# Third attention layer: queries and keys in two rounded parts, scores as three rounded products

## The chip, the cores and the metric

The kernel runs on one core of a Trainium2 chip. The metric is the time of one execution on the device in microseconds (us). The engines are TensorE (PE, with its weight loads as PEld), VectorE (DVE), ScalarE (ACT), GpSimd (POOL) and SyncE (SP), which issues most DMAs. Each engine works through its own queue in order.

## What is computed

The reference is two blocks one after the other on a sequence of 512 tokens with 1024 features. The first merges a state-space branch, a gated recurrence and an attention over a memory; the second is a chain of four layers, of which the third is a latent attention (`mla_branch`), the one that is changed. Cut to what matters:

```python
def mla_branch(h, w_in, q_norm, kv_norm, w_uq, w_ukv, w_out):      # 16 heads
    c_q, c_kv, k_rope, z = split(h @ w_in, [768, 1024, 1056])
    q  = (rmsnorm(c_q, q_norm) @ w_uq)      # per head 64 plain + 32 rope columns
    kv = (rmsnorm(c_kv, kv_norm) @ w_ukv)   # per head 64 key + 64 value columns
    q = concat(q[..., :64], rope(q[..., 64:]))
    k = concat(kv[..., :64], rope(k_rope) for every head)          # 96 wide
    o = causal_attention(q, k, kv[..., 64:], scale=96 ** -0.5)
    return (o * silu(z)) @ w_out
```

The scores are causal: query block n (128 queries) sees (n + 1) * 128 keys, so a head has four score tiles of 128 x 128, 128 x 256, 128 x 384 and 128 x 512.

## The kernel before, in words

The whole program is one Python trace; a scheduler puts each engine's instructions into an order by their place in the program and by what is ready. Large products are made with rounded operands: a value is copied by ACT into a rounded type (`fp32r`, the high part) and DVE subtracts that from the value to get the low part; the product is then high x high + high x low + low x high. For weights this is `wsplit` (L311 to L323): `wfetch` (L302) loads 128 x 1024 into one of three staging buffers `wf`, ACT casts into `wh` (L317), DVE subtracts into `wl` (L318). There are seven pairs `wh`/`wl`, taken in turn through the counter `nw`, so a cast waits until PE has finished with the weights of seven loads before. For activations it is `split` (L467; without a scale the copy is L471 and the subtraction L472). All matmuls that are not transposes go through the helper `mm` (L272), so their line is L277 (L275 when an order is asked for). Plain two-tensor operations of this layer go through the helper `tt`, so their line is L1803.

PSUM has four banks `g` (products and scores, handed out in turn by `gb`) and four banks `t` (transposes, probabilities times values). The working memory has 36 slots of 128 x 512 fp32 (`st`, `Slots`), handed out first in, first out, and eight rounded tiles `rt`.

The third attention layer is `mla` (L1801). Its part in front makes the latents, the rotated shared key `kr`, and two sets of key tiles `kt[s][e]` (s: even or odd head pair, e: head of the pair) in `st` slots: POOL clears 32 unused rows, ACT copies the rope rows (L1855 to L1858). Then 8 head pairs c follow. `up(c)` makes the pair's keys (`w_uk`, ACT copies at L1883 and L1884 empty the bank), for every even c a rope tile of two pairs (`w_uq[8 + t]`; two products with the rope tables and a shuffle on DVE, L1892), and the queries (`w_uq[c]`, ACT copies at L1901, and DVE adds the two rope halves into the query tile). `scores(c)` makes per head four fp32 matmuls query x key into the `g` banks, DVE adds the causal mask and takes the maximum (L1936), ACT takes the exponential (L1940), DVE normalises (L1943). One head's four scores are eight fp32 records. `core(c)` transposes the probabilities of pair c (L1959, copied at L1961), makes the scores of pair c + 1 in between, and multiplies with the values. `weave` mixes `core(c)` with fillers: the gate product of the pair (`gate`, 24 matmuls of 512 columns, L1236 and L1237 empty its bank), `up(c + 2)`, and once the second half of the values. After pair 7 the output projection `layer_out("w_co")` takes eight weight loads.

## Time and profile before

| | |
|---|---|
| median of 3 runs | 1915.02 us (1912.07 to 1915.43) |
| profiled execution, its own time | 1914.73 us |
| its span, first to last instruction | 1913.0 us |
| PE busy | 1863.3 us (97%) |
| PE weight loads busy | 1515.8 us (79%) |
| DVE busy | 1299.9 us (68%) |
| ACT busy | 893.1 us (47%) |
| POOL busy | 60.4 us (3%) |
| mean granted TensorE clock | 0.996 of full speed |

Busy time of an engine is the time covered by its instructions. Matmuls are pipelined: a record's end is modelled and reaches over the start of the next one, so the spacing of starts says what PE is held for, and the length of one record says more than that. An fp32 matmul leaves two records, a rounded one leaves one. A timeline row merges several records of one kind: its length goes from the start of the first to the end of the last, and the shape is that of the first. "Idle before" is the time in which an engine did nothing in front of an instruction, and the arrow names what ended it.

### The profile page before, as it was taken

How to read it: one execution, taken by the hardware profiler on the slowest of the kernel's cores; microseconds unless marked ns; L12 is line 12 of the kernel's file. 1: busy time of each engine (PE TensorE's matmuls, PEld its weight loads, DVE VectorE, ACT ScalarE, POOL GpSimd, SP SyncE). 2: the span in 40 equal slices, each digit the busy share in tenths (PEclk: the TensorE clock that was granted, in tenths of full speed). 3: DMA queues.
4: the chain of work that ended last, by engine and by line, in shares of the span. 5: the costliest groups of instructions: out<-in, count | busy, mean ns of one | idle time of the engine just before them, and what ended most of it. 6: DMA issues, size and time to landing. Idle time of an engine off the chain costs nothing. (4 is left out here: it accounts for less than half of the span.)

```text
span 1913.0 us, 26324 instructions
## 1 busy us (share of the span) xinstructions
PE 1863.3 (97%) x9843; PEld 1515.8 (79%) x9843; DVE 1299.9 (68%) x2579; ACT 893.1 (47%) x1666; POOL 60.4 (3%) x93
## 2 busy tenths in 40 slices
PE   8999999999999999999999999999999999999998
PEld 7778787888888788778778888888887677788887
DVE  7776777757467797765655965787664776758553
ACT  5554545454376644432334454465544555534231
POOL 0010001100000000000001010000000000000000
PEclk9999999999999999999999999999999999999999
DMA  5343324323332436533469554232323122333421
GB/s 184 106 136 97 120 96 121 116 68 118 88 102 82 129 124 204 188 103 119 159 233 309 152 191 130 66 120 77 102 100 100 53 64 67 99 121 110 133 77 44
DMA packets 99202, 229.91 MB, mean 120 GB/s; under 512 B 18081, under 2 KB 38977, under 8 KB 99074
## 3 DMA queue, kind: packets, MB, share of 16 engines
q1 hardware_dynamic: 86192, 216.85, 35.5%
q0 software_dynamic: 2544, 6.00, 1.1%
q10 hardware_dynamic: 10338, 5.38, 1.0%
q8 instruction: 77, 1.26, 0.3%
q14 instruction: 51, 0.42, 0.1%
HBM read 200.28 MB, written 26.35 MB: 118 GB/s over the span
## 5 line engine op out<-in xcount | busy, mean ns | idle before, releaser
L277 PE MATMUL g<-rt,wh 128*128 128x512 f32 (+1 forms) x3664 | 1097.4, 382 | 7.0 <-ACT rt L471 4.2
L277 PEld LDWEIGHTS g<-rt,wh 128*128 128x128 f32 x3664 | 669.0, 189 | 141.0 <-ACT st L1940 5.3
L277 PE MATMUL g<-rt,wl 128*128 128x512 f32 (+1 forms) x1816 | 682.0, 380 | 0.0
L317 ACT CAST wh<-wf 128x1024 fp32r<-128x1024 f32 (+2 forms) x300 | 301.0, 1011 | 469.0 <-PE g L277 337.9
L318 DVE TENSOR_TENSOR wl<-wf,wh 128x1024 fp32r<-128x1024 f32 (+2 forms) x300 | 349.8, 1173 | 241.9 <-ACT wh L317 228.1
L277 PEld LDWEIGHTS g<-rt,wl 128*128 128x128 f32 x1816 | 343.2, 189 | 63.2 <-issue 2.2
L277 PE MATMUL g<-wh,rt 128*128 128x512 f32 x992 | 310.2, 393 | 0.9 <-DVE rt L475 0.7
L277 PEld LDWEIGHTS g<-wh,rt 128*128 128x128 f32 x992 | 185.8, 189 | 40.5 <-DVE rt L475 1.0
L277 PE MATMUL g<-wl,rt 128*128 128x512 f32 x496 | 193.4, 390 | 0.0
L277 PEld LDWEIGHTS g<-wl,rt 128*128 128x128 f32 x496 | 93.1, 188 | 19.5 <-issue 0.3
L277 PE MATMUL t<-st 128*64 128x64 f32 (+8 forms) x746 | 76.8, 274 | 8.0 <-DVE st L720 3.8
L665 DVE SCALAR_TENSOR_TENSOR st<-g,pc,st 128x511 f32<-128x511 f32 (+2 forms) x108 | 80.0, 745 | 5.6 <-ACT st L662 5.0
L1260 DVE TENSOR_TENSOR st<-st 128x512 f32<-128x512 f32 (+4 forms) x180 | 76.5, 468 | 6.7 <-PE t L1415 5.5
L275 PE MATMUL t<-st 128*64 128x128 f32 (+4 forms) x788 | 72.9, 299 | 4.9 <-ACT st L708 4.9
L275 PEld LDWEIGHTS t<-st 128*64 128x64 f32 (+1 forms) x788 | 55.0, 145 | 20.0 <-issue 10.5
L277 PEld LDWEIGHTS t<-st 128*64 128x64 f32 (+3 forms) x746 | 44.3, 142 | 32.0 <-issue 18.0
L1196 DVE TENSOR_TENSOR st<-g,st 128x512 f32<-128x512 f32 x32 | 22.0, 689 | 60.1 <-ACT st L1195 59.9
L277 PE MATMUL g<-st 128*128 128x256 f32 (+2 forms) x192 | 56.5, 426 | 5.5 <-DVE st L1237 2.4
L744 ACT ACTIVATE st<-st 128x128 f32<-128x128 f32 x128 | 41.8, 394 | 37.2 <-POOL st L740 37.2
L474 ACT ACTIVATE rt<-st 128x512 fp32r<-128x512 f32 x52 | 35.5, 712 | 49.9 <-DVE st L1621 16.3
L720 DVE TENSOR_TENSOR st<-st,t 128x512 f32<-128x512 f32 x68 | 45.2, 681 | 17.0 <-issue 5.8
L1195 ACT ACTIVATE st<-g 128x512 f32<-128x512 f32 x32 | 19.1, 596 | 76.3 <-PE g L277 76.3
(301 smaller groups left out, 1836.7 us busy)
## 6 DMA issues: line engine op xcount, KB each, us to landing
wf<-in_w_xbc SPq DMA_DIRECT2D x24, 512.0 KB
wf<-in_w_gt SPq DMA_DIRECT2D x24, 512.0 KB
wf<-in_w_z SPq DMA_DIRECT2D x16, 512.0 KB
st<-acsD SPq DMA_DIRECT2D x32, 256.0 KB
wf<-in_w_bs SPq DMA_DIRECT2D x16, 512.0 KB
wf<-in_w_lx SPq DMA_DIRECT2D x12, 512.0 KB
wf<-in_w_lg SPq DMA_DIRECT2D x12, 512.0 KB
wf<-in_w_bl SPq DMA_DIRECT2D x16, 384.0 KB
```

Of the source, the lines that this page charges most:

```text
L275: r = self.nc.tensor.matmul(out=out, lhsT=lhsT, rhs=rhs, start=start, stop=stop)
L277: r = self.nc.tensor.matmul(out=out, lhsT=lhsT, rhs=rhs, start=start, stop=stop)
L317: a = nc.scalar.copy(wh, wf)
L318: b = nc.vector.tensor_tensor(out=wl, in0=wf, in1=wh.bitcast(F32), op=ALU.subtract)
L474: nc.scalar.activation(hi, src, AF.Copy if isinstance(scale, float) else AF.Identity, scale=scale)
L665: nc.vector.scalar_tensor_tensor(out=out[:, d:], in0=ps[:, :512 - d], scalar=pcs(f"{n}w{j}", t), in1=out[:, d:], op0=ALU.mult, op1=ALU.add)
L720: tt = lambda o, a, b, op: nc.vector.tensor_tensor(out=o, in0=a, in1=b, op=op)
L744: nc.scalar.activation(m[:, j * P:(j + 1) * P], m[:, j * P:(j + 1) * P], AF.Exp, bias=self.nacs[:, c, h:h + 1])
L1195: nc.scalar.activation(y[:, c], ps, AF.Square, scale=1.0 / 32, accum_out=ss[:, i, n:n + 1])
L1196: nc.vector.tensor_tensor(out=y[:, c], in0=ps, in1=pg[n], op=ALU.mult)
L1260: tt = lambda o, a, b, op: V.tensor_tensor(out=o, in0=a, in1=b, op=op)
```

## The change

The keys and queries of the third attention layer are no longer fp32 tiles in `st` slots. Each is kept as a high and a low rounded part. The place for them is taken from the ring of weight buffers: the counter `nw` becomes a list `W` of pairs, four pairs are taken off its front when the key tiles are made and put back after the last pair of heads, and the other three pairs serve the weight loads in between. Pair s of the lent ones holds the two heads' keys of set s (high part in `wh`, low part in `wl`, 512 columns for each head), pairs 2 and 3 the queries, which so also have two sets in place of slots taken as needed. All copies into them become `split` (a copy on ACT and a subtraction on DVE); the rope halves are added once for two pairs, in place, and then split into each query tile. Each score becomes three rounded matmuls into one bank: high x high, query high x key low, query low x key high.

```diff
--- before.py
+++ after.py
@@ -219,7 +219,8 @@
         self.wf = [p.tile([P, 1024], F32, name=f"wf{j}") for j in range(self.NWF)]
         self.wh = [p.tile([P, 1024], F32R, name=f"wh{j}") for j in range(self.NWS)]
         self.wl = [p.tile([P, 1024], F32R, name=f"wl{j}") for j in range(self.NWS)]
-        self.nw = self.nf = 0
+        self.W = list(zip(self.wh, self.wl))
+        self.nf = 0
         rt = p.tile([P, self.NR, 4, 512], F32R, name="rt")
         st = p.tile([P, self.NS, 512], F32, name="st")
         self.R = Slots(rt, self.NR)
@@ -308,12 +309,15 @@
             self.after(r, self.last_dma)
         return wf

+    def wpair(self):
+        t = self.W.pop(0)
+        self.W.append(t)
+        return t
+
     def wsplit(self, wf, n=1024):

         nc = self.nc
-        wh = self.wh[self.nw % self.NWS][:, :n]
-        wl = self.wl[self.nw % self.NWS][:, :n]
-        self.nw += 1
+        wh, wl = (t[:, :n] for t in self.wpair())
         a = nc.scalar.copy(wh, wf)
         b = nc.vector.tensor_tensor(out=wl, in0=wf, in1=wh.bitcast(F32), op=ALU.subtract)
         if self.fence and self.exempt <= 0:
@@ -364,8 +368,7 @@

         nc, nk = self.nc, len(xs)
         wf = self.wfetch(src, nk * m).rearrange("p (k m) -> p k m", k=nk)
-        w = self.wh[self.nw % self.NWS][:, :nk * m * 2].rearrange("p (k e m) -> p k e m", k=nk, e=2)
-        self.nw += 1
+        w = self.wpair()[0][:, :nk * m * 2].rearrange("p (k e m) -> p k e m", k=nk, e=2)
         nc.scalar.copy(w[:, :, 0], wf)
         nc.vector.tensor_tensor(out=w[:, :, 1], in0=wf, in1=w[:, :, 0].bitcast(F32), op=ALU.subtract)
         seq = [(0, 0)] + [(k, 1) for k in range(nk)] + [(k, 0) for k in range(1, nk)]
@@ -1850,12 +1853,15 @@
         kr = self.tb()
         self.mm(kr, ktab[:, 512:640], ks, True, True)

-        kt = [[S.get(), S.get()] for _ in range(2)]
+
+        lent = [self.W.pop(0) for _ in range(4)]
+        kt, qt = ([[[t[:, 512 * e:512 * e + 512] for t in lent[s]] for e in range(2)] for s in r]
+                  for r in (range(2), range(2, 4)))
         for s in range(2):
-            nc.gpsimd.memset(kt[s][0][96:128], 0.0)
-            nc.gpsimd.memset(kt[s][1][0:32], 0.0)
-            nc.scalar.copy(kt[s][0][64:96], kr[64:96])
-            nc.scalar.copy(kt[s][1][32:64], kr[32:64])
+            for e, (z, r) in enumerate(((slice(96, 128), slice(64, 96)), (slice(0, 32), slice(32, 64)))):
+                for part in kt[s][e]:
+                    nc.gpsimd.memset(part[z].bitcast(F32), 0.0)
+                self.split(*(part[r] for part in kt[s][e]), kr[r])
         S.put(ks, *kts)

         ch, cl = [R.get(), R.get()], [R.get(), R.get()]
@@ -1867,7 +1873,7 @@
         for a in cv:
             S.put(*a)
         cs = self.pairs(ch, cl)
-        vt, qs, rot = {}, {}, {}
+        vt, rot = {}, {}

         def values(n):
             vt[n] = [S.get() for _ in range(4)]
@@ -1880,8 +1886,8 @@

             b = self.gb()
             self.gemm_fm(b, I["w_uk"][c], cs[6:])
-            nc.scalar.copy(kt[c % 2][0][0:64], b[0:64])
-            nc.scalar.copy(kt[c % 2][1][64:128], b[64:128])
+            for e, n in enumerate((slice(0, 64), slice(64, P))):
+                self.split(*(part[n] for part in kt[c % 2][e]), b[n])
             t = c // 2
             if c % 2 == 0:
                 yield
@@ -1891,15 +1897,15 @@
                 tt(rot[t][0], b, tabs[0], ALU.mult)
                 nc.vector.stream_shuffle(rot[t][1], b, [(j + 16) % 32 for j in range(32)])
                 tt(rot[t][1], rot[t][1], tabs[1], ALU.mult)
+                tt(rot[t][0], rot[t][0], rot[t][1], ALU.add)
+                S.put(rot[t].pop())
             yield
             b = self.gb()
             self.gemm_fm(b, I["w_uq"][c], cs[:6])
-            q = qs[c] = [S.get(), S.get()]
-            x, y = (r[64 * (c % 2):64 * (c % 2) + 64] for r in rot[t])
-            for e in range(2):
-                n, r = (slice(0, 64), slice(64, P))[::1 - 2 * e]
-                nc.scalar.copy(q[e][n], b[n])
-                tt(q[e][r], x, y, ALU.add)
+            x = rot[t][0][64 * (c % 2):64 * (c % 2) + 64]
+            for q, n, r in zip(qt[c % 2], (slice(0, 64), slice(64, P)), (slice(64, P), slice(0, 64))):
+                self.split(*(part[n] for part in q), b[n])
+                self.split(*(part[r] for part in q), x)
             if c % 2:
                 S.put(*rot[t])
             yield
@@ -1931,7 +1937,9 @@
                         w = (n + 1) * P
                         sc = self.gb()[:, :w]
                         scs.append(sc)
-                        self.mm(sc, qs[c][e][:, n * P:(n + 1) * P], kt[c % 2][e][:, :w], True, True)
+                        for a, b in ((0, 0), (0, 1), (1, 0)):
+                            self.mm(sc, qt[c % 2][e][a][:, n * P:(n + 1) * P], kt[c % 2][e][b][:, :w],
+                                    a + b == 0, a == 1)
                         tt(sc[:, n * P:], sc[:, n * P:], mask, ALU.add)
                         nc.vector.tensor_reduce(out=t[:, n:n + 1], in_=sc, axis=AX.X, op=ALU.max)
                     ns = slice(2 * n2, 2 * n2 + 2)
@@ -1941,7 +1949,6 @@
                 nc.vector.reciprocal(t[:, 8:12], t[:, 4:8])
                 for n in range(4):
                     nc.vector.tensor_scalar(es[n], es[n], t[:, 8 + n:9 + n], None, op0=ALU.mult)
-                S.put(qs[c][e])
                 yield

         def core(c):
@@ -2007,7 +2014,8 @@
             if c == 3 or c == 7:
                 S.put(*vt[c // 4])
         R.put(*ch, *cl)
-        S.put(ms, *tabs, *kt[0], *kt[1])
+        S.put(ms, *tabs)
+        self.W = lent + self.W
         self.layer_out("w_co", self.pairs(yr[:2], yr[2:]), 2)
         R.put(*yr)
 
```

## Rows read from the trace of the kernel before

**Rows 1.** The page: span, and busy time of each engine.
```profile
span 1913.0 us, 26324 instructions
PE 1863.3 (97%) x9843; PEld 1515.8 (79%) x9843; DVE 1299.9 (68%) x2579; ACT 893.1 (47%) x1666; POOL 60.4 (3%) x93
```

**Rows 2.** Busy time by stretch; span; PE, PEld, DVE, ACT, POOL; clock; DMA, GB/s.
```profile
1601.90:1622.90 21.00, 20.53 (x104) 14.78 (x102) 14.84 (x39) 11.06 (x27) 0.00 (x0) 1.00 0.22 75
1622.90:1647.90 25.00, 24.53 (x121) 18.05 (x119) 19.88 (x46) 13.85 (x31) 0.00 (x0) 1.00 0.26 85
sum 188.20, PE 182.17 PEld 133.33 DVE 136.59 ACT 102.11 POOL 2.15; mean PE 20.24 PEld 14.81 DVE 15.18 ACT 11.35 POOL 0.24
```

**Rows 3.** Waits between 1490 and 1680 us: total us, times, longest us.
```profile
ACT wh L317 <- PE g L277: 33.8, 21, 4.3
PEld g L277 <- ACT st L1940: 8.8, 12, 2.0
PE g L277 <- DVE st L1237: 2.4, 5, 0.5
```

**Rows 4.** Groups by shape, PE, 1400 to 1700 us: xcount, busy us, mean ns, idle.
```profile
L277 PE MATMUL g<-st 128*128 128x512 f32 x32 | 17.7, 635 | 2.7 <-DVE st L1237 2.4 <-ACT st L1901 0.3
L277 PE MATMUL g<-st 128*128 128x384 f32 x32 | 13.0, 489 | 1.6 <-ACT st L1940 1.6
L277 PE MATMUL g<-st 128*128 128x256 f32 x32 | 9.7, 384 | 0.0
L277 PE MATMUL g<-st 128*128 128x128 f32 x32 | 6.3, 278 | 0.7 <-ACT st L1901 0.7
```

**Rows 5.** Timeline of PE, from several stretches: start us, length us, engine, line, shape.
```profile
1500.64 2.40 PE L277 MATMUL g<-st 128*128 128x128 f32 x8 [0.71 <-ACT st L1901]
1495.68 1.52 PE L277 MATMUL g<-rt,wh 128*128 128x512 f32 x6
...
1299.73 0.52 PE L277 MATMUL g<-rt 128*128 128x256 f32 x3
1310.97 0.96 PE L277 MATMUL g<-rt 128*128 128x128 f32 x6
```

**Rows 6.** Groups by shape, PE, whole span.
```profile
L277 PE MATMUL g<-rt 128*128 128x256 f32 x96 | 18.7, 301 | 0.3 <-DVE rt L1698 0.2
L277 PE MATMUL g<-rt 128*128 128x128 f32 x32 | 6.2, 274 | 0.5 <-DVE rt L1698 0.5
```

**Rows 7.** Groups by shape, DVE and ACT, 1490 to 1680 us.
```profile
L1803 DVE TENSOR_TENSOR st<-st 64x512 f32<-64x512 f32 x16 | 11.0, 686 | 0.4
...
L1901 ACT COPY st<-g 64x512 f32<-64x512 f32 x16 | 9.3, 579 | 2.7 <-PE g L277 2.4
```

**Rows 8.** Timeline at the start of the layer's head pairs, DVE and PE.
```profile
1499.31 2.10 DVE L1803 TENSOR_TENSOR st<-st 64x512 f32<-64x512 f32 x3
1503.41 0.74 PE L277 MATMUL g<-rt,wh 128*128 128x512 f32 x2 [0.37 <-ACT st L1940]
...
1515.31 0.91 PE L277 MATMUL g<-st 128*128 128x384 f32 x2 [1.60 <-ACT st L1940]
```

**Rows 9.** Timelines of ACT and PE around 1602 us.
```profile
1600.78 1.18 ACT L1901 COPY st<-g 64x512 f32<-64x512 f32 x2
...
1603.76 1.13 PE L277 MATMUL g<-st 128*128 128x512 f32 x2
```

**Rows 10.** Timeline in a later round, DVE and PE.
```profile
1637.48 1.22 DVE L318 TENSOR_TENSOR wl<-wf,wh 128x1024 fp32r<-128x1024 f32 x1
...
1639.35 1.12 PE L277 MATMUL g<-st 128*128 128x512 f32 x2 [0.47 <-DVE st L1237]
```

**Rows 11.** Busy time in an earlier stretch, columns as in the second group.
```profile
669.20:717.00 47.80, 47.80 (x242) 39.56 (x244) 45.53 (x145) 18.98 (x40) 0.00 (x0) 1.00 0.37 123
```

**Rows 12.** Timelines of ACT and PE: a weight cast and the first use.
```profile
1616.88 1.05 ACT L317 CAST wh<-wf 128x1024 fp32r<-128x1024 f32 x1 [1.06 <-PE g L277]
...
1667.47 2.10 PE L277 MATMUL g<-rt,wh 128*128 128x512 f32 x8
```

## Prediction

> **What bounds the kernel now.** I read the page's header first, then the busy table by stretch for the third attention layer, then its waits, and last the matmul records by shape and a few timelines. The page says that TensorE (PE) is busy for 97% of the span and VectorE (DVE) for 68% [rows 1]. The table by stretch says the same of the layer that is changed: between 1490 and 1678.2 us PE is busy for 182.2 of 188.2 us, so all its idle time is 6.0 us, while DVE has 136.6 us and ScalarE (ACT) 102.1 us of work [rows 2]. So the layer ends when PE has issued its matmuls; what counts is how much PE work goes away, and whether DVE and ACT can still hand PE its operands and empty its banks in time. The reader is to see in [rows 2] that DVE's share is uneven: 14.8 of 21.0 us in one round of the layer, 19.9 of 25.0 us in the next, because a rope tile (`w_uq[8+t]`) is made for two head pairs at once. The waits say which releases reach PE today: score banks that ACT's exponentials have to empty (8.8 us of waits in the weight-load queue, partly behind running matmuls) and a bank that DVE's gate product empties (2.4 us in 5 waits) [rows 3]. ACT's waits for PE before a weight cast (33.8 us) are ACT waiting for a weight buffer, and cost PE nothing [rows 3].
>
> **Part 1, what PE gains.** The 64 score matmuls (8 head pairs, 2 heads, 4 query blocks of widths 128, 256, 384 and 512) are plain fp32 today, and the trace holds 128 records of them, two for each: 17.7 + 13.0 + 9.7 + 6.3 = 46.7 us of busy time, which counts the modelled tail of every short run [rows 4]. What PE is really held for is the spacing. The first head's eight records run from start to modelled end in 2.40 us [rows 5]. After the change the same head takes twelve records, three for each width, each with rounded operands. Their spacing is in the trace: six rounded 512-wide records take 1.52 us, the last of them 0.39 us long like its neighbours, so (1.52 - 0.39) / 5 = 0.226 us each; three 256-wide ones (second attention layer) take 0.52 us with 0.30 us for one, so 0.11 us each; six 128-wide ones take 0.96 us with 0.27 us for one, so 0.14 us each [rows 5, 6]. There is no rounded 384-wide record; it lies between 0.11 and 0.226 us, and I take the middle, 0.168 us, since its width is in the middle. One head then takes 3 x (0.226 + 0.168 + 0.11 + 0.14) = 1.93 us and 0.16 us of tail (what the last record is longer than its spacing), 2.09 us in place of 2.40 us. With 16 heads that is 16 x 0.31 = 5.0 us. With the 384-wide record at either end it is 16 x (0.31 + 0.17) = 7.7 us or 16 x (0.31 - 0.17) = 2.2 us. The gain is this small because the narrow blocks gain little or lose: a 128-wide score needs two short records now and three then.
>
> The Trainium skill, "FP8 and Floating Point Precision", section TensorE Precision Notes, says that a true fp32 product takes four passes through the array. Three passes in place of four would by that rule take a quarter off 16 x 2.40 = 38.4 us, 9.6 us, an estimate from the page; the rows agree with it at 512 columns alone, where fp32 is nearly four times as long as one rounded record, and not at 128.
>
> **Part 2, what DVE and ACT get.** For each of the 8 head pairs the key part gets 2 subtractions, the query part 2, the rope part 2, each of 64 x 512; the 2 rope additions of 64 x 512 go, and one of 128 x 512 comes for every two pairs. The subtractions are not in the trace; the nearest row is the rope addition of the same shape, 686 ns (16 of them, 11.0 us), which I take for the 128 x 512 ones too, their columns being the same [rows 7]. So DVE gets (48 - 16 + 4) x 0.686 = 24.7 us more. ACT gets 16 copies of 64 x 512 for the rope parts, at 579 ns as the query copies take, 9.3 us [rows 7]. DVE then has 136.6 + 24.7 = 161.3 us of work in about 184 us, 88%; ACT 111 us. By round: the two rounds of [rows 2] together have 34.7 us of DVE work in 46.0 us and would get 12 subtractions less 4 additions plus one, 6.2 us, so 40.9 us, 89%; nearly all of it in the second, which alone would be full. Nothing here sets the end by itself; the cost lies in latency, in three places.
>
> *The start of the layer.* Pair 0 has no attention work in front of it that could cover it. DVE does three rope additions in a row (2.10 us), and PE has stood idle for 0.71 us before its first score and waits again for 0.37 and 1.60 us after it [rows 5, 8]. After the change a head's query is complete only when its copy has been followed by its subtraction, and DVE has one addition and four subtractions (5 x 0.69 = 3.4 us) where it had two additions (1.4 us) per pair. Bounds: nothing if the weight splits that now stand in DVE's queue move away, 2 x 2.0 = 4.0 us if both pairs 0 and 1 are exposed. I take 2.5 us, since PE already waits here.
>
> *The bank of a query product.* The four `g` banks go round, and the widest score of a head is written into the bank that the query product or the gate had four uses earlier. Today two ACT copies empty the query's bank (end at 1601.96) and the score that takes it starts at 1603.76, 1.8 us later, or 1.5 us with faster scores in front of it [rows 9]. Two subtractions of 0.69 us are added behind the copies, in a queue in which mask additions and maxima of 0.3 to 0.7 us stand; the release moves by 0.7 to 2.5 us. So the wait is 0 to 1.0 us in those rounds where the query product stands right in front of the scores (3 of the 6 rounds that make queries); I take 0.5 us each, 1.5 us. How such a wait looks is already there: a weight split of 1.22 us stands in front of the gate product on DVE, and PE stands idle 0.47 us for the bank [rows 10].
>
> *Everything else on a DVE queue that is 88% full.* Behind each subtraction stand the mask addition, the maximum and the normalisation, for which the exponentials, then the transposes wait. Bounds: nothing (the page has a stretch with DVE busy for 45.5 of 47.8 us in which PE is never idle [rows 11]) to 1.2 us in each of 6 rounds, the length of one weight split in front of a link of the chain [rows 10]. I take 0.3 us, 1.8 us, nearer to the row without idle time.
>
> **Part 3, the ring of weight buffers.** Seven pairs of buffers become three until the layer's last scores. A cast then waits for the matmuls of three loads earlier instead of seven. The last gate's weights are cast at 1616.88 and used at 1667.47, 50.6 us ahead [rows 12]; with three buffers the lead is some two products and the attention work between them, at the least 5 us of matmuls, and a cast with its subtraction takes 1.05 + 1.22 = 2.3 us [rows 10, 12]. I take nothing; what hides it is that lead, and if it is gone the price is up to 2.3 us at each of the layer's loads. The output projection finds all seven buffers back, four of them free as soon as the last scores are done, a good 10 us before it starts. The freed `st` slots (four for keys, two for each query, one rope slot earlier) remove waits if anything; I count nothing. The eight memsets on POOL are on an engine that is 3% busy, long before the keys are needed [rows 1].
>
> **The sum.** The profiled execution took 1914.73 us with a span of 1913.0 us, so 1.7 us lie outside it; it is 0.3 us under the median of 1915.02 us. From it: 1914.7 - 5.0 + 2.5 + 1.5 + 1.8 = 1915.5 us. I forecast 1915.5 us: no change that can be told. (About 0.2%, 3.8 us, is what a measurement of this kernel can tell from no change.)
>
> **The rivals.**
> *DVE hides all of it (faster).* The subtractions fall into DVE's present idle time (51.6 us in the layer) and PE's gain arrives nearly whole: 1914.7 - 5.0 = 1909.7 us. For it speaks the stretch with DVE at 95% and a full PE [rows 11]; against it, that PE already waits at the start of the layer [rows 8]. Chance 0.24.
> *Three passes for four (clearly faster).* If a rounded product costs exactly a quarter of an fp32 one at all widths, the gain is a quarter of 16 x 2.40 us and the time 1914.7 - 9.6 = 1905 us without new waits. The 128-wide records speak against it [rows 5]. Chance 0.04; this is what the rule of the skill's page would give.
> *DVE's queue becomes the bound of the rounds (slower).* Place: the emptying of the query bank and the gate bank, behind weight splits and subtractions on one in-order queue. Price: 1.5 us in each of 6 rounds and 4.0 us at the start: 1914.7 - 5.0 + 4.0 + 9.0 = 1922.7 us. It decides for slower from 0.9 us per round on (1913.7 + 6 x 0.9 = 1919.1). For it speaks the round that would be full [rows 2]; against it, that its neighbour is at 77%. Chance 0.26.
> *The ring starves PE (slower).* 2.3 us at 6 of the loads on top of the forecast: 1915.5 + 13.8 = 1929 us. Against it speak the leads above. Chance 0.06.
>
> **How the numbers follow.** The forecast, 1915.5 us with its own range of 1911.5 to 1918.5 us, has the remaining 0.40. Faster by over 0.2% needs a time under 1911.2 us: 0.24 + 0.04 = 0.28. Slower by over 0.2% needs one over 1918.8 us: 0.26 + 0.06 = 0.32. The range reaches down to 1908.5, below the first rival, and up to 1924, past the third; left out are the second and the fourth and a little of the others' ends, under 0.2 together.
>
> **What would show it.** Twelve records per head at the spacings above, in about 2.1 us, show part 1 right. DVE's busy time in the layer up by about 25 us and ACT's by 9 us show part 2's sizes. PE's idle time in the layer, 6.0 us now, should come out at 11 to 13 us, with the new waits before scores and released by DVE's subtractions; if it stays at 6 the first rival holds, and if it passes 16 the third does. Waits of PE for a weight cast or its subtraction would show the ring. The prediction is wrong if the order of work changes far from the layer, which none of these terms holds.

## The result and the profile after

The changed kernel took 1928.32 us (median of 4 runs, 1925.56 to 1930.49) where the kernel before took 1914.77 us beside it. The ratio is 1.0065 with an interval of 1.0048 to 1.0081: slower by 13.5 us by the medians and 12.4 by the ratio, outside the range that was given. Where the two ways differ for a run below, both ends are given. The profiled execution took 1930.49 us. Lines of the kernel moved by one at `mm` (L278) and by three for the layer's small helpers (`tt` is L1806), and by more behind the scores: exponential L1948, scaled maximum L1946.

The page of the kernel after, which answers to [rows 1]:

```profile
span 1928.8 us, 26490 instructions
PE 1868.8 (97%) x9907; PEld 1529.2 (79%) x9907; DVE 1326.7 (69%) x2619; ACT 901.6 (47%) x1682; POOL 63.0 (3%) x97
```

The share of PE is still 97%, and the 64 records more are the ones forecast. To see where the 15.8 us of span went, I cut the layer at the start of each head pair's first product with the values, and read the busy table by stretch of both kernels, columns as in [rows 2] (PE, PEld, DVE, ACT, POOL, then the clock). Kernel before, from the start of the layer's scores to the products of the last pair:

```profile
1499.50:1524.90 25.40, 22.39 (x100) 15.85 (x99) 20.28 (x57) 15.81 (x40) 0.00 (x0) 1.00 0.23 77
1524.90:1551.10 26.20, 25.70 (x121) 18.38 (x120) 20.89 (x52) 13.83 (x34) 0.00 (x0) 1.00 0.21 66
1551.10:1571.00 19.90, 19.52 (x101) 14.45 (x100) 13.05 (x33) 9.57 (x24) 0.00 (x0) 1.00 0.14 42
1571.00:1601.50 30.50, 30.03 (x145) 22.62 (x144) 18.60 (x48) 15.67 (x36) 0.00 (x0) 1.00 0.22 69
1601.50:1622.40 20.90, 20.43 (x103) 14.71 (x102) 14.74 (x37) 11.46 (x27) 0.00 (x0) 1.00 0.22 76
1622.40:1647.40 25.00, 24.53 (x119) 18.07 (x118) 19.88 (x48) 13.37 (x30) 0.00 (x0) 1.00 0.26 85
1647.40:1661.80 14.40, 13.93 (x74) 9.64 (x73) 10.03 (x25) 7.45 (x20) 0.00 (x0) 1.00 0.20 53
1661.80:1678.20 16.40, 16.15 (x83) 11.72 (x83) 13.62 (x36) 10.28 (x25) 2.15 (x2) 1.00 0.51 156
```

Kernel after, the same cut, and the sum from 1490 us on:

```profile
1500.60:1532.50 31.90, 24.94 (x117) 19.55 (x115) 26.06 (x66) 17.98 (x44) 0.00 (x0) 0.89 0.20 59
1532.50:1559.30 26.80, 24.65 (x129) 19.04 (x128) 21.32 (x51) 15.00 (x34) 0.00 (x0) 1.00 0.19 55
1559.30:1579.90 20.60, 19.64 (x106) 15.19 (x105) 15.56 (x40) 10.20 (x26) 0.00 (x0) 1.00 0.16 52
1579.90:1613.70 33.80, 30.60 (x156) 24.17 (x155) 23.47 (x55) 18.53 (x41) 0.00 (x0) 1.00 0.20 59
1613.70:1634.30 20.60, 19.64 (x108) 15.19 (x107) 15.56 (x41) 10.17 (x27) 0.00 (x0) 1.00 0.15 42
1634.30:1662.90 28.60, 26.00 (x129) 20.36 (x128) 21.80 (x51) 14.40 (x34) 0.00 (x0) 0.94 0.24 81
1662.90:1678.70 15.80, 14.87 (x87) 11.34 (x86) 13.92 (x35) 9.72 (x23) 0.00 (x0) 1.00 0.37 123
1678.70:1694.70 16.00, 16.00 (x87) 12.34 (x86) 15.70 (x34) 12.88 (x28) 1.62 (x2) 1.00 0.54 168
sum 204.70, PE 186.94 PEld 145.93 DVE 161.10 ACT 114.07 POOL 1.62; mean PE 20.77 PEld 16.21 DVE 17.90 ACT 12.67 POOL 0.18
```

The last mark lies at 1694.7 in place of 1678.2 us, 16.5 us later, so the whole loss is in here. PE's idle time (stretch less busy) went from 6.0 us to 204.70 - 186.94 = 17.8 us. Of the 11.8 us more, 4.0 lie in the start (3.0 to 7.0), 6.5 in the three rounds that make a rope tile (second, fourth and sixth line: 0.5 to 2.2, 0.5 to 3.2, 0.5 to 2.6) and 1.3 in the other four. The remaining 16.5 - 11.8 = 4.7 us are busy time, which by the forecast should have gone down. A part of that is the clock: two lines have a granted clock under 1.00. PE's waits from 1490 to 1695 us and those of ACT that matter here:

```profile
ACT wh L474 <- DVE st L1806: 11.7, 4, 4.2
...
PE g L278 <- ACT st L1948: 11.2, 15, 1.5
ACT wh L474 <- DVE wl L475: 10.3, 9, 1.7
...
PE g L278 <- DVE wl L475: 3.4, 5, 1.3
...
PE g L278 <- DVE st L1240: 2.1, 6, 0.5
```

In [rows 3] the bank of the gate was the largest of PE's waits (2.4 us); now it is a score bank that the exponential has to empty, 15 times, and 5 times the bank of a key or query product that a subtraction still reads. (The wait names L475, but the products that wait are high x high and need no low part.) No line has PE waiting for a weight cast. Behind the start alone, from 1532.5 us on in the kernel after and from 1524.9 us on in the kernel before, PE's waits for exponentials are:

```profile
PE g L278 <- ACT st L1948: 8.2, 12, 1.5
...
PE g L277 <- ACT st L1940: 0.4, 1, 0.4
```

There the gate's bank has 2.1 us against 2.4 us before, and the subtractions have 0.5 us in 2 places.

**The start, instruction by instruction.** Timeline rows of DVE, ACT and PE of the kernel after:

```profile
1501.37 0.69 DVE L475 TENSOR_TENSOR wl<-st,wh 64x512 fp32r<-64x512 f32 x1 [0.68 <-ACT wh L474]
1502.09 0.68 DVE L475 TENSOR_TENSOR wl<-g,wh 64x512 fp32r<-64x512 f32 x1
1502.70 0.67 DVE L475 TENSOR_TENSOR wl<-st,wh 64x512 fp32r<-64x512 f32 x1
1503.34 0.30 DVE L1806 TENSOR_TENSOR g<-g,st 128x128 f32<-128x128 f32 x1
1503.75 0.69 DVE L475 TENSOR_TENSOR wl<-g,wh 64x512 fp32r<-64x512 f32 x1
1504.47 0.29 DVE L1944 TENSOR_REDUCE tiny<-g 128x1 f32<-128x128 f32 x1
...
1506.19 0.37 ACT L1948 ACTIVATE st<-g,tiny 128x128 f32<-128x128 f32 x1 [1.83 <-DVE tiny L1946]
...
1502.09 0.30 PE L278 MATMUL g<-wh,wh 128*128 128x128 f32 x1 [1.08 <-ACT wh L474]
...
1504.49 0.50 PE L278 MATMUL g<-wh,wh 128*128 128x512 f32 x1 [0.92 <-DVE wl L475]
...
1506.70 0.73 PE L278 MATMUL g<-rt,wh 128*128 128x512 f32 x2 [1.24 <-ACT st L1948]
```

Four subtractions stand on DVE ahead of the first maximum (1504.47 us), three of them from the start of the first score on. Before, the first score started at 1500.64 us [rows 5] and PE's next product at 1503.41 [rows 8]; now it is 1502.09 and 1506.70. The scores start 1.45 us later and their first bank comes free 3.3 us later. The second head pair goes through the same once more (PE waits of 0.68 and 1.27 us for L475, and 1.29 us for L1948, up to 1520.87 us), and then this happens:

```profile
1516.00:1519.00 3.00, 1.57 (x8) 1.13 (x9) 2.88 (x9) 1.08 (x5) 0.00 (x0) 1.00 0.20 79
1519.00:1525.80 6.80, 5.51 (x15) 4.28 (x15) 4.88 (x17) 2.25 (x9) 0.00 (x0) 0.50 0.01 2
...
1655.50:1658.90 3.40, 3.40 (x10) 2.66 (x9) 1.25 (x3) 1.92 (x4) 0.00 (x0) 0.50 0.02 5
```

These are again rows of the busy table of the kernel after. Behind a stretch in which PE was busy for 1.57 of 3.00 us the granted clock is 0.50 for 6.8 us, the 1.2 GHz level in place of 2.4, and once more for 3.4 us in the sixth round. PE's busy time there is 5.51 + 3.40 = 8.9 us; the 512-wide products start 0.43 us apart there and 0.23 us apart elsewhere, so I estimate that half of it, 4.5 us, is the price of the lower level; that is about the whole surplus of busy time. The kernel before has no such stretch in the layer. The Trainium skill, "TensorE: Matmul & The Clock Gate", Part 1, says that the throttled level is the default and that activity releases it; the rows agree: the clock falls behind PE's gaps, is back at 1.00 behind 6.80 us of which PE was busy for 5.51, and does not fall at the start when the gaps there are filled (start_filled, below).

**A later round.** Timeline rows of DVE, PE and ACT of the kernel after, in the round that [rows 10] showed of before:

```profile
1651.06 1.23 DVE L322 TENSOR_TENSOR wl<-wf,wh 128x1024 fp32r<-128x1024 f32 x1 [0.32 <-ACT wh L321]
1652.20 0.68 DVE L1240 SCALAR_TENSOR_TENSOR st<-st,g 128x512 f32<-128x512 f32 x1
1652.80 0.28 DVE L1944 TENSOR_REDUCE tiny<-g 128x1 f32<-128x128 f32 x1
...
1652.94 0.51 PE L278 MATMUL g<-wh,wh 128*128 128x512 f32 x1 [0.50 <-DVE st L1240]
...
1653.52 0.40 PE L278 MATMUL g<-wh,wl 128*128 128x512 f32 x1
...
1654.39 0.37 ACT L1948 ACTIVATE st<-g,tiny 128x128 f32<-128x128 f32 x1 [1.54 <-DVE tiny L1946]
...
1654.90 0.73 PE L278 MATMUL g<-rt,wh 128*128 128x512 f32 x2 [0.99 <-ACT st L1948]
```

And what followed [rows 10] in the timelines of the kernel before, ACT and PE:

```profile
1639.94 0.37 ACT L1940 ACTIVATE st<-g,tiny 128x128 f32<-128x128 f32 x1 [0.65 <-DVE tiny L1938]
...
1640.45 0.73 PE L277 MATMUL g<-rt,wh 128*128 128x512 f32 x2
```

In both kernels the 512-wide score waits 0.5 us for the gate's bank. Before, the score took 1.12 us from 1639.35 on [rows 10], the first exponential stood at 1639.94, and PE's next product went on at 1640.45 without a pause. Now the three records are done at 1653.52 + 0.40 = 1653.92, 0.98 us after their start, but the first maximum stands behind a weight split and the gate on DVE, the exponential comes at 1654.39, and PE is idle for 0.99 us. From one start to the next product it was 1.10 us and is 1.96 us: what PE saves at the score it waits for behind it, and more.

No subtraction of a key or query stands in these rows. The same two waits, 0.51 and then 1.00 us, stand in an earlier round of a kernel that makes no low part at all (no_low_parts, below):

```profile
1543.73 0.73 PE L278 MATMUL g<-rt,wh 128*128 128x512 f32 x2 [1.00 <-ACT st L1947]
```

So this wait belongs to the faster score and the order of work on DVE, not to the low parts.

### The profile page after: what moved, and what is told of

It is laid out like the page before. It is cut to its first block, busy times and chain, and to the rows that moved or that the text cites. A ratio compares the mean times of both kernels' runs of the same rounds, so it can differ in the third digit from the quotient of the medians.

```text
span 1928.8 us, 26490 instructions
## 1 busy us (share of the span) xinstructions
PE 1868.8 (97%) x9907; PEld 1529.2 (79%) x9907; DVE 1326.7 (69%) x2619; ACT 901.6 (47%) x1682; POOL 63.0 (3%) x97
## 5 line engine op out<-in xcount | busy, mean ns | idle before, releaser
L278 PE MATMUL g<-rt,wh 128*128 128x512 f32 (+1 forms) x3664 | 1100.5, 383 | 15.9 <-ACT st L1948 9.1
L278 PEld LDWEIGHTS g<-rt,wh 128*128 128x128 f32 x3664 | 671.0, 190 | 150.1 <-ACT st L1948 12.7
L278 PE MATMUL g<-rt,wl 128*128 128x512 f32 (+1 forms) x1816 | 683.7, 380 | 0.0
L278 PEld LDWEIGHTS g<-rt,wl 128*128 128x128 f32 x1816 | 344.3, 190 | 63.2 <-issue 2.2
L278 PE MATMUL g<-wh,rt 128*128 128x512 f32 x992 | 310.8, 394 | 0.7 <-DVE rt L478 0.7
L278 PEld LDWEIGHTS g<-wh,rt 128*128 128x128 f32 x992 | 186.1, 189 | 40.1 <-DVE rt L478 1.0
L278 PE MATMUL g<-wl,rt 128*128 128x512 f32 x496 | 193.6, 391 | 0.0
L278 PEld LDWEIGHTS g<-wl,rt 128*128 128x128 f32 x496 | 93.4, 188 | 19.7 <-issue 0.3
L278 PE MATMUL t<-st 128*64 128x64 f32 (+8 forms) x746 | 78.5, 277 | 6.9 <-DVE st L723 3.3
L278 PEld LDWEIGHTS t<-st 128*64 128x64 f32 (+3 forms) x746 | 45.6, 144 | 28.2 <-issue 15.6
L478 DVE SCALAR_TENSOR_TENSOR rt<-st,rt 128x512 fp32r<-128x512 f32 x52 | 38.5, 762 | 18.2 <-ACT rt L477 16.2
```

The lines of the kernel that those rows point to most:

```text
L278: r = self.nc.tensor.matmul(out=out, lhsT=lhsT, rhs=rhs, start=start, stop=stop)
L478: nc.vector.scalar_tensor_tensor(out=lo, in0=src, scalar=scale, in1=hi.bitcast(F32), op0=ALU.mult, op1=ALU.subtract)
```

## The experiments

The rivals behind them: the ring of weight buffers (B, where an expectation uses letters); the amount of work on DVE and ACT in their in-order queues; and the banks of the key and query products, which an ACT copy and a DVE subtraction now empty one behind the other, twice (C). Beside these, whether PE bounds the layer at all. A mark below is the start of a pair's first product with the values; before it is 1524.9 us for the first and 1678.2 for the last, after it is 1532.5 and 1694.7. Diffs are against the changed kernel, except the first.

**ring3_alone.** The kernel before, with four of the seven weight buffers set aside in the layer and used for nothing.

```diff
+        lent = [self.W.pop(0) for _ in range(4)]
         kt = [[S.get(), S.get()] for _ in range(2)]
...
         S.put(ms, *tabs, *kt[0], *kt[1])
+        self.W = lent + self.W
```

> The kernel before, with nothing of the change but the ring: the four pairs of weight buffers are taken out of the ring at the same place and put back at the same place, and nobody uses them. Queries, keys and scores stay fp32. Theory A (the changed kernel loses its 13.5 us to in-order queues: the added copies and subtractions delay what empties the score banks): the ring of three alone costs 0 to 1.5 us, so 1914 to 1917 us. Theory B (the ring of three starves TensorE of split weights): most of the loss is here already, 1922 to 1930 us.

1916.15 us, ratio 1.0003 [0.9993, 1.0012]. The ring costs nothing that can be told.

**no_low_parts.** No low part of keys and queries is made; the three products all read high parts.

```diff
-                self.split(*(part[n] for part in q), b[n])
-                self.split(*(part[r] for part in q), x)
+                nc.scalar.copy(q[0][n], b[n])
+                nc.scalar.copy(q[0][r], x)
...
-                            self.mm(sc, qt[c % 2][e][a][:, n * P:(n + 1) * P], kt[c % 2][e][b][:, :w],
+                            self.mm(sc, qt[c % 2][e][0][:, n * P:(n + 1) * P], kt[c % 2][e][0][:, :w],
```

> The changed kernel without the subtractions for queries and keys: each score is still three rounded products with the same shapes, but all three read the high parts, and no low part is made (this part of the computation is left out). TensorE, the ring and ScalarE's copies keep their work; VectorE loses 52 subtractions, some 33 us. Theory A (VectorE's added work delays the release of banks and the start of the layer): 1913 to 1918 us. Theory A2 (ScalarE's copies of the rope halves wait in their queue for VectorE's rope addition, and the exponentials behind them): only part of it comes back, 1919 to 1924 us. Theory B (ring): 1925 us or more.

1916.76 us, ratio 1.0014 [1.0000, 1.0028]. The low parts cost 10 to 12 us. What is as telling: with all subtractions for keys and queries gone from DVE and the cheaper scores kept, the kernel is still not faster than before. From its waits, PE waits for exponentials in 10 places:

```profile
PE g L278 <- ACT st L1947: 6.5, 10, 1.0
```

That was 2.3 us in 3 places before; behind the first mark it is 4.8 us against 0.4. The gain at the scores turns into this wait.

**one_product.** Only high x high is made; two of the three score products are left out.

```diff
-                        for a, b in ((0, 0), (0, 1), (1, 0)):
+                        for a, b in ((0, 0),):
...
```

> The changed kernel with only the high x high product of each score (the two others are left out); all splits, waits and the ring stay. TensorE loses 128 records, by the spacings some 20 us. If TensorE is what the layer is bound by: 1906 to 1911 us. If the chain through VectorE and ScalarE sets the pace of the layer now: under half of the 20 us comes off, 1919 us or more.

1925.26 us, ratio 1.0046 [1.0030, 1.0062]. By the spacings below 16 x 1.25 = 20 us of PE work went, and the time fell by 3.1 (medians) to 3.6 us (ratio), within overlapping intervals. PE does not bound the layer. The two views here are of an execution of 1920.89 us, one of the two quickest of seven. The largest of its waits there:

```profile
PE g L278 <- ACT st L1948: 21.1, 12, 2.8
```

And the start in the busy table:

```profile
1500.50:1532.20 31.70, 23.15 (x82) 17.36 (x82) 24.70 (x63) 17.15 (x43) 0.00 (x0) 0.73 0.16 48
```

The last row shows a reservation: the start, where PE has less to do, has a clock of 0.73 against 0.89, so part of the 20 us was taken back that way.

**rope_high_on_pool.** The high copies of the rope halves on GpSimd in place of ACT.

```diff
-                self.split(*(part[r] for part in q), x)
+                nc.gpsimd.tensor_copy(q[0][r], x)
+                tt(q[1][r], x, q[0][r].bitcast(F32), ALU.subtract)
```

> The changed kernel with one move: the high parts of the 16 rope halves are copied by GpSimd in place of ScalarE, so that ScalarE's queue never stands behind VectorE's rope addition. Theory A2 (that queue is where rounds 3 and 5 and part of the start lose their time; ScalarE sits 11.7 us in 4 waits for the rope addition): 5 to 8 us come back, 1920 to 1923 us. Theory A (VectorE's amount of work): no change or slower, 1926 us or more, since VectorE's work is the same and its subtractions now wait for a slower copy.

1927.65 us, ratio 1.0064 [1.0049, 1.0079]: no change. The wait for the rope addition (11.7 us above) no longer stands in ACT's queue there, and PE's waits for exponentials are still 9.7 us in 14 places, so that wait alone is not the cause.

**no_rope_low.** The low parts of the rope halves of the queries are zero; only the subtractions that read no bank go.

```diff
-                self.split(*(part[r] for part in q), x)
+                nc.scalar.copy(q[0][r], x)
+                if c < 2:
+                    nc.gpsimd.memset(q[1][r].bitcast(F32), 0.0)
```

> The changed kernel without the 16 subtractions that make the low part of the queries' rope rows; these rows are zero in the low part (that part of the computation is left out). These subtractions read no bank, so no score bank is held by them; they are a third of the added subtractions. Theory Q (it is the amount of VectorE's work that costs): a third of the 11.5 us that all low parts cost, 1924 to 1925 us. Theory C (it is the banks that are now emptied by a copy and a subtraction, one behind the other): 1926.5 us or more.

1926.24 us, ratio 1.0056 [1.0041, 1.0071] against 1916.64. 1.7 us back by the ratio and 3.9 by the medians; the intervals overlap.

**bank_early.** ACT copies the product whole out of the bank; the parts are made from the copy.

```diff
+            v = S.get()
+            nc.scalar.copy(v, b)
...
-                self.split(*(part[n] for part in q), b[n])
+                self.split(*(part[n] for part in q), v[n])
```

> The changed kernel, but the product of the keys and that of the queries is first copied as a whole (128 x 512) by ScalarE into a slot, and the high and low parts are made from the slot. The bank is free after one copy; VectorE's work is the same, ScalarE gets 16 copies more, some 9 us. Theory C (banks): 4 us or more come back, 1924 us or less. Theory Q (amount of VectorE's work), or a chain that is longer at the start: 1927 us or more.

1924.78 us, ratio 1.0048 [1.0030, 1.0066]. 3.3 to 5.4 us back, the intervals still overlapping, for 8.7 us more of ACT (122.7 us in the layer).

**rope_all_on_pool.** The second table product of the rope, the addition of its halves and both parts of them on GpSimd.

```diff
-                tt(rot[t][1], rot[t][1], tabs[1], ALU.mult)
-                tt(rot[t][0], rot[t][0], rot[t][1], ALU.add)
+                gt(rot[t][1], rot[t][1], tabs[1], ALU.mult)
+                gt(rot[t][0], rot[t][0], rot[t][1], ALU.add)
+                rot[t].append(S.get())
+                nc.gpsimd.tensor_copy(rot[t][2].bitcast(F32R), rot[t][0])
+                gt(rot[t][1].bitcast(F32R), rot[t][0], rot[t][2], ALU.subtract)
...
-                self.split(*(part[r] for part in q), x)
+                for part, y in zip(q, x):
+                    nc.gpsimd.tensor_copy(part[r], y)
```

> The changed kernel with the rope rows moved to GpSimd: the second table product, the addition, the split (once for two pairs) and eight copies into the query parts. VectorE loses 16 subtractions, 4 products and 4 additions, some 16.5 us, ScalarE 16 copies, some 9 us; TensorE, the banks and the ring are as in the changed kernel. Theory Q: about half of the 11.5 us come back, 1921 to 1923 us. Theory C: 1925 us or more, since the banks are emptied as before. If GpSimd is too slow for the queries, waits of TensorE for GpSimd show and it is slower than 1928 us.

1930.38 us, ratio 1.0078 [1.0061, 1.0095]. The busy table from 1490 us to the last mark:

```profile
sum 203.50, PE 185.07 PEld 144.54 DVE 152.40 ACT 101.08 POOL 40.24; mean PE 61.69 PEld 48.18 DVE 50.80 ACT 33.69 POOL 13.41
```

ACT has what it had before (102.1 us), DVE 8.7 us less than after, and nothing is gained. Less work on these two alone does not bring the time back. The reservation: at the start PE now waits 3.44 us for GpSimd's copies and the clock is 0.75 against 0.89, so this version has a price of its own there. Behind the start it has none that the waits show, and still gains nothing: from the first mark to the last it takes 160.4 us, where after takes 162.2, 1.7 of them the clock's in the sixth round.

**Orders: up1_first, copies_first, max_first, three_moves, no_low_max_first.** The first makes all of pair 1's keys and queries ahead of pair 0's scores; the second makes both copies out of a bank before both subtractions; the third puts the second half's mask additions behind the first half's scaled maximum; the fourth is all three; the last is the third on top of no_low_parts.

```diff
-        weave(scores(0), [up(1)], 2)
+        run(up(1))
+        run(scores(0))
```

```diff
+    def halves(self, parts):
+        for hi, lo, src in parts:
+            self.nc.scalar.copy(hi, src)
+        for hi, lo, src in parts:
+            self.nc.vector.tensor_tensor(out=lo, in0=src, in1=hi.bitcast(F32), op=ALU.subtract)
...
```

```diff
+                        if done2 is not None:
+                            self.after(m, done2)
...
```

> The changed kernel with the keys and queries of pair 1 made in the program before the scores of pair 0, so that TensorE has their products to do while pair 0's parts are made. The start of the layer loses 7 us to the kernel before (first product with the values at 1532.5 in place of 1524.9 us), 3.4 us of it at half the clock. If the start is lost because TensorE has nothing to do while parts are made: 3 to 5 us come back, 1923 to 1925 us. If VectorE is the bound of the start (26 of 32 us busy): under 1.5 us, 1927 us or more.

> The changed kernel with one change of order: of a key or query product both high copies stand in front of both subtractions. In the trace of the changed kernel ScalarE's second copy out of a bank waits until VectorE's subtraction out of the same bank is over (10.3 us in 9 waits), with the exponentials queued behind it. Theory D (the two engines take turns at one bank, and that holds ScalarE's queue): these waits go away and 3 us or more come back, 1925 us or less. Theory E (the order of masks and maxima on VectorE holds the first exponential): under 1.5 us, 1927 us or more.

> The changed kernel with one order added on VectorE: the mask of a head's third and fourth score comes after the scaled maxima of the first two. In the changed kernel the third score's mask and maximum stand in front of them, the first exponential starts about 1 us later than it could, and TensorE waits 1.0 to 1.2 us for its bank in front of the key product in most rounds (11.2 us of waits for the exponential in all). Theory E: 3 to 5 us come back, 1923 to 1925 us. Theory D: under 1.5 us.

> The changed kernel with both changes of order, and pair 1's keys and queries in front of the scores of pair 0 in the program. If the three places are separate, their parts add up: 1928 less some 3 + 4 + 1.5, about 1919 to 1921 us. If they are one chain through VectorE, no more than the best of them alone, 1923 us or more. Faster than the kernel before (1914 us or less) is not expected.

> The kernel without low parts (no subtraction for queries and keys, all three products read the high parts, so that part of the computation is left out) with the order of masks and maxima as in the run of that change. Without the low parts the time was 1916.8 us, so TensorE's gain of some 5 us was not there either. Theory E: it was given back at the first exponential, and comes with the order: 1911 to 1914 us. Otherwise the layer is bound elsewhere: 1916 us or more.

| | us | ratio |
|---|---|---|
| up1_first | 1927.02 | 1.0057 [1.0039, 1.0075] |
| copies_first | 1931.26 | 1.0080 [1.0057, 1.0103] |
| max_first | 1933.42 | 1.0094 [1.0074, 1.0114] |
| three_moves | 1929.40 | 1.0073 [1.0050, 1.0096] |
| no_low_max_first | 1915.02 | 1.0004 [0.9993, 1.0015] |

No order brings it back. The last row has the time of before, but it makes no low parts; against no_low_parts it is about 2 us lower, with overlapping intervals. Of the others up1_first alone lies under after, by 1.5 to 3.1 us, again within the intervals; max_first was to give 3 to 5 us back and is, if anything, slower. In copies_first ACT's waits for a subtraction out of the same bank (10.3 us above) are no longer among its larger waits; PE waits 9.2 us for exponentials (11.2 in after) and 1.9 for subtractions (3.4), but 3.7 for the gate's bank (2.1). In max_first, where the maxima were to be earlier, PE waits 10.0 us for exponentials and 6.9 for subtractions. Each order moves part of the wait to another link. The Trainium skill, "PSUM — Partial Sum Buffer", section PSUM bank collisions raise a hardware error, says that two engines may use one bank at a time if they keep to different groups of 32 partitions; the two halves here do so, and the kernel still puts its copies and subtractions one behind the other (9 waits, 10.3 us). copies_first takes most of these waits away and is not faster; both halves read at once was not tried.

**no_bank_low.** The opposite of no_rope_low: the low parts that are read out of a bank are zero, those of the rope are made.

```diff
-                self.split(*(part[n] for part in q), b[n])
+                nc.scalar.copy(q[0][n], b[n])
+                if c < 2:
+                    nc.gpsimd.memset(q[1][n].bitcast(F32), 0.0)
```

> The changed kernel without the 32 subtractions that read a bank (low parts of the 64 key rows and of the 64 plain query rows; these rows of the low parts are zero, that part of the computation is left out). The rope rows keep their low part. It is the complement of the run without the rope's low parts, which gave 1.7 us back of the 11.5 us. Theory C (copy and subtraction one behind the other out of one bank, before a score or the next user of the bank may go on): most of the 11.5 us come back, 1917 to 1920 us. If the two thirds go by number only: 1920.5 us or more.

1920.24 us, ratio 1.0022 [1.0010, 1.0034] against 1915.01. 8.2 to 8.3 us are back (13.5 - 5.2 by the medians, 12.4 - 4.2 by the ratio), for 32 subtractions; no_rope_low gave 1.7 to 3.9 for 16 of the same length, and the two together are about the 10 to 12 us of no_low_parts. One subtraction so costs 0.26 us when it reads a bank and 0.1 to 0.24 when not: some two fifths of its length or less, and by this no sharp difference between the two kinds. Where they do differ is the start, which is then as before:

```profile
1499.50:1525.10 25.60, 21.66 (x115) 17.61 (x115) 20.44 (x56) 17.52 (x44) 0.00 (x0) 1.00 0.20 66
```

The first mark is 1525.1 us against 1524.9, the last 1684.0 against 1678.2. So without the subtractions from the banks, 8 of the 12 of pairs 0 and 1, the start loses nothing, and the 4 to 5 us that remain lie in the rounds. Without the other 4, those of the rope, its mark is 1529.2 us; with all 12 and the banks emptied by one copy (bank_early) it is 1529.7.

**start_filled.** 48 useless 512-wide products into a free bank among the scores of pairs 0 and 1, to keep PE busy there.

```diff
+                        if c < 2:
+                            d = self.tb()
+                            for k in range(3):
+                                self.mm(d, ch[0][:, k, :P], ch[0][:, k], k == 0, k == 2)
```

> The changed kernel with three matmuls of 512 rounded columns, of no use, in front of each of the 16 scores of pairs 0 and 1, into transpose banks that are free then; 48 x 0.23 = 11 us of TensorE time, about the 7 to 8 us that it idles there and some more. Theory F (half the clock at the start of the layer, 6.8 us in the changed kernel's trace, comes from TensorE's idle stretches in front of it): no stretch at half clock between 1500 and 1530 us, and the time goes up by less than the added work that finds no idle time, 1926 to 1930 us. If the clock falls there all the same: 1931 us or more.

1928.11 us, ratio 1.0069 [1.0054, 1.0084]: the same time with 48 x 0.226 = 10.8 us more work on PE. The start of this kernel:

```profile
1499.50:1530.20 30.70, 30.32 (x154) 24.79 (x153) 27.70 (x71) 16.23 (x42) 0.00 (x0) 1.00 0.13 41
```

PE is busy throughout, the clock is 1.00, and the first mark is at 1530.2 us, earlier than after's 1532.5 in spite of the added work. So the lower clock follows from PE's gaps, and by this execution costs some of the start. With the full clock the stretch is still 5 us longer than before, but here PE, with the added products, is busy for 30.3 of 30.7 us and DVE for 27.7, and either can set its length. That DVE's queue sets the start in the changed kernel is argued, not shown.

**start_fp32** and **start_fp32_bank_early.** Pairs 0 and 1 are made as before (fp32 tiles, fp32 scores), the other six as after; the second version adds bank_early for those six.

```diff
-                self.split(*(part[n] for part in kt[c % 2][e]), b[n])
+                if c < 2:
+                    nc.scalar.copy(k0[c][e][n], b[n])
+                else:
+                    self.split(*(part[n] for part in kt[c % 2][e]), b[n])
...
+                        if c < 2:
+                            self.mm(sc, q0[c][e][:, n * P:(n + 1) * P], k0[c][e][:, :w], True, True)
+                        for a, b in ((0, 0), (0, 1), (1, 0)) if c > 1 else ():
```

> The changed kernel with pairs 0 and 1 made as in the kernel before (fp32 keys and queries in slots, one fp32 product for each score), pairs 2 to 7 as in the changed kernel. If the start is lost because parts have to be made with nothing to cover them, and because the clock falls behind that: 6 to 8 us come back, 1920 to 1922 us, with no stretch at half clock around 1520 us. If the later rounds are what costs: under 3 us, 1925 us or more.

> The same, and for pairs 2 to 7 the key and query products are copied as a whole into a slot first, so that the bank is free after one copy. The run with that alone gave 3.3 us back, 2.8 of them at the start; so some 0.5 to 2 us less than the run before in this list. Faster than the kernel before would need the rounds to lose nothing: not expected, 1917 us or more.

1921.14 us, 1.0038 [1.0024, 1.0051], and 1918.94 us, 1.0016 [1.0006, 1.0026]. The first has its first mark at 1524.8 us, as before, and no stretch at the lower clock in the layer; it is 5 to 7 us better than after (12.4 - 7.3 by the ratio, 13.5 - 6.1 by the medians). Its last mark is 7.2 us later than before: that is what the rounds cost by themselves, of which an early copy out of the bank saves 2 to 4 us, with intervals that just touch. Both are slower than before still; I found no version that beats it. From the first mark to the last, in the busy table of the first and of the second:

```profile
1524.80:1685.40 160.60, 150.16 (x787) 116.31 (x786) 127.42 (x302) 90.83 (x209) 0.33 (x1) 1.00 0.24 77
...
1525.90:1683.50 157.60, 149.11 (x785) 115.71 (x784) 126.79 (x304) 97.34 (x220) 1.42 (x2) 1.00 0.26 80
```

The kernel before takes 153.3 us for this stretch and no_low_parts 156.5. So of the 7.3 us that the rounds lose, 3.2 are there without any subtraction, and the early copy takes back 3.0 of the other 4.1 with DVE's work left as it was (127 us) and ACT's raised. In the rounds this speaks against the amount of work on DVE and for the time that the banks are held. Each of these figures is from one execution; which link of the chain the early copy shortens is not shown, and copies_first says that it is not the taking of turns at the bank alone.

## Why the prediction was wrong

**Part 1, right as a size, wrong as a gain.** The spacings came as forecast. The rows of a timeline of PE in the kernel after, of one head's 128- and 256-wide scores:

```profile
1512.27 0.22 PE L278 MATMUL g<-wh,wh 128*128 128x128 f32 x1
...
1512.56 0.33 PE L278 MATMUL g<-wh,wh 128*128 128x256 f32 x1
...
1512.96 1.25 PE L1966 MATMUL t<-ident,st 128*128 128x128 f32 x10
```

Three 128-wide records hold PE for 0.29 us (0.42 forecast), three 256-wide ones for 0.40 (0.33), 384-wide ones follow at 0.18 us each where they are not stopped (0.168; 1650.65 to 1651.18 us), 512-wide ones at 0.23: 0.29 + 0.40 + 0.53 + 0.68 = 1.90 us for a head, 1.93 forecast. (One reading beside the sum was off: two fp32 records of 512 columns take 1.13 us with 0.16 of tail [rows 9], so they are a little over four times one rounded record, not nearly four.) The step that failed is the one before it, "the layer ends when PE has issued its matmuls". It was read from PE's 182.2 of 188.2 us [rows 2], and that a busy PE leaves little idle time does not say that less work would end earlier. In the round of [rows 10] the fp32 score was just as long as the chain from the gate's bank to the first exponential, so no wait was seen. The -5.0 us came out as nothing: no_low_parts is 2 to 3 us above before with the cheaper scores and all subtractions gone, and no_low_max_first, the best of that kind, has the time of before. Nor do they show in PE's busy time, which without the clock's 4.5 us is that of before: at each stop the modelled tail of the last record lies open, as at 1652.94 us, where three records are busy for 0.98 us and not 0.68.

**The start, mis-sized: 2.5 us forecast, 4.0 at most, 5 to 7 measured** (first mark +7.6 us; start_fp32 gains 5 to 7). The place and the sign were right [rows 8]. Three things were not in the term. It counted four subtractions on DVE for each pair and left out the two of the keys, 2 x 0.69 us, which part 2 has. It had PE wait for a finished query; but of the 4.0 us of added idle time 2.9 are high x high products that wait for a bank which a subtraction still reads, and 1.0 is for exponentials, whose maxima queue behind four subtractions. And it had no term for the clock, which falls behind the gaps so made; by the rows above I estimate up to 3 us of the start for it.

**The rounds, mis-sized: 1.5 + 1.8 - 5.0 us forecast with PE's gain, 6 to 7 measured** (start_fp32: 6.1 to 7.3 us, last mark +7.2; that kernel has the cheaper scores in six of eight pairs). They hold the loss where the prediction looked for it: the round of 25.0 us that it called nearly full became 28.6 us, 1.7 of them clock, and its neighbour of 21.0 us did not change (20.9 to 20.6). But the query's bank, for which 1.5 us were taken, has 0.5 us of PE's waits there; the waits that this term foresaw came at the start. The term that was mis-sized is "everything else": 1.8 us forecast, while PE's waits for exponentials rose from 0.4 to 8.2 us. Without any subtraction they are still 4.8 us (no_low_parts): 4.4 of the 7.8 us more are the gain at the scores turned into waits, the step that failed in part 1. The price in a round that makes a rope tile was 1.7 to 2.7 us more of idle time, where the terms gave 0.3 to 0.8, and the row chosen as the nearest for "everything else", a stretch with DVE at 95% and PE never idle [rows 11], has no chain from a score over a maximum to an exponential that PE waits for.

**Part 2's sizes, right.** DVE in the layer rose by 161.1 - 136.6 = 24.5 us (24.7 forecast) and ACT by 12.0 (9.3 forecast; the 16 copies took 9.9 us, the rest is mostly weight casts that now fall into the stretch). The subtraction of a rope half took 684 ns and its copy 618 ns; 686 and 579 had been taken from [rows 7].

**Part 3, right.** ring3_alone shows the ring at 0.0003 of the time, and no PE wait names a weight cast.

**The rivals.** The third, DVE's queue as the bound of the rounds (1922.7 us), had the sign, and DVE's in-order queue as the cause; it too took off 5.0 us for PE that did not arrive, and without that its sum is 1927.7 us. That this lies near the 1928.3 measured is in part luck, for its place in the rounds was not the right one: it named the query's and the gate's bank, which have 0.5 us of new waits and 2.1 us against 2.4, while the banks that PE waits for are those that the exponentials empty. Its own sign, PE idle over 16 us in the layer, came (17.8). What is shown is that making the low parts costs 10 to 12 us (no_low_parts) and that the gain at the scores does not arrive. What stays open is how the 10 to 12 us divide between banks held longer and DVE's queue: at the start PE's waits name the banks, but bank_early brings back only part; in the rounds the early copy brings back 3.0 of 4.1 us, and rope_all_on_pool nothing. Every change of order moved the waits elsewhere, and no run isolates one link.

## What to carry to other kernels

An engine at 97% is the bound only if its next operands are ready early; before a saving is booked, ask which chain (here gate, maximum, exponential, bank) ends at the same moment, because the saving is then a wait. As far as these runs go, an added step is to be priced by the chain that it lengthens, copy then subtraction then the next user, above all where nothing else can run, rather than by the share of its engine alone. Where gaps open in front of TensorE, its granted clock belongs into the sum.

## What the hardware showed that I had not expected

- TensorE's clock fell to its 1.2 GHz level inside a layer in which it was busy for over 90% of the time: 6.8 us behind a stretch with 1.57 of 3.00 us busy, with 512-wide products 0.43 us apart in place of 0.23. Filled with useless products the same stretch kept 1.00, and the program took the same time (start_filled).
- A 128 x 512 addition or product took GpSimd 1374 ns (rope_all_on_pool), twice VectorE's 684. VectorE's own instructions grew in that kernel: the scaled maximum of 128 x 2 from 160 to 248 ns, the 512-wide normalisation from 481 to 546 ns. Of the 24 instructions of about 0.69 us that left it (16.5 us), only 8.7 us showed in its busy time; that the growth of the others is the cause is my reading.
